# A batched matmul with a subtraction: transposes ahead of the subtract, single first loads, fewer zero matmuls, a reordered list of transfers

## Chip, cores, metric

One core of a Trainium2 chip. The metric is the device time of one execution in microseconds (us). Every run told of here is a program on one core; differences are judged with a 95% interval. "Faster" or "slower" means by more than 2%.

## The reference

```python
def setup_inputs():
    batch, m, k, n = 16, 512, 1024, 768
    return {
        "x": np.random.randn(batch, m, k).astype(np.float32),
        "weight": np.random.randn(k, n).astype(np.float32),
        "sub_value": np.random.randn(batch, m, n).astype(np.float32),
    }

def reference(x, weight, sub_value):
    return (np.matmul(x, weight) - sub_value).astype(np.float32)
```

## The kernel before

The 8192 rows of x are 64 tiles of 128. A tile is loaded as float32, cast to float16 (ScalarE, tile 1 on VectorE), transposed, multiplied with the weights into PSUM, and the subtrahend is taken off by VectorE, in place in the buffer from which the output is written. Of every six tiles, two (a "pair") are transposed by VectorE in 16 blocks, four by TensorE against an identity. SyncE issues all transfers, from one list in one order:

```python
SEGMENTS = [(0, 2), (2, 6)] + [(at, 8) for at in range(8, 64, 8)]   # which rows share a partition
N16P, NXTP = 2, 1        # buffers of a pair: cast, transposed
IDLE = 34
LEAD_TURN = 5
PER = 6

TRANSFERS = [            # kind (x, weights, subtrahend, output), first tile, tiles
    ('x', 0, 2), ('x', 2, 2), ('w', 0, 2), ('w', 2, 2), ('x', 4, 4), ('s', 0, 2), ('s', 2, 6),
    ('x', 8, 4), ('x', 12, 4), ('s', 8, 8), ('x', 16, 8), ('s', 16, 8), ('x', 24, 8),
    ('o', 0, 2), ('o', 2, 6), ('s', 24, 8), ('s', 32, 8), ('x', 32, 8), ('x', 40, 8),
    ('o', 8, 8), ('o', 16, 8), ('s', 40, 8), ('x', 48, 2), ('x', 50, 6), ('o', 24, 8),
    ('s', 48, 8), ('x', 56, 8), ('s', 56, 8), ('o', 32, 8), ('o', 40, 8), ('o', 48, 8),
    ('o', 56, 5), ('o', 61, 2), ('o', 63, 1),
]
# ... (cut)
    def idle(n):
        pe.add(lambda: nc.tensor.ldweights(idle_w, tile_position=(0, 0)), [(counter["idle"], 2)])
        for _ in range(n):
            pe.add(lambda: loaded_matmul(po_b[:, NPO - 1, 0], idle_w, idle_x, start=True, stop=True))
# ... (cut)
    idle(IDLE)           # and one more, which waits for the identity
# ... (cut)
    for mi in range(n_mt):
        for c in range(n_c):
            # ... (cut: transposes on TensorE at fixed places)
            matmuls(mi, c)
        for t in casts.get(mi, []):
            cast(t)
        finish(mi)                                   # VectorE: the subtract of tile mi
        for t in range(mi + 1, n_mt):
            if t in ON_DVE and mi == t - LEAD_TURN:
                waiting += transposes_dve(t)         # VectorE: 16 blocks of a pair
        for f in waiting[:PER]:
            f()
        del waiting[:PER]
```

The matmuls of a tile wait for its transposes and for a free one of three PSUM buffers, that is for the subtract of three tiles before.

Of the kernel before, what the change touches and what calls it, by code (L numbers as in the profile page):

```python
# [10 lines left out]
F32 = mybir.dt.float32  # L11
F16 = mybir.dt.float16

SEGMENTS = [(0, 2), (2, 6)] + [(at, 8) for at in range(8, 64, 8)]
NX, NSO = 16, 32
N16, NXT, NPT, NPO = 4, 4, 2, 3
N16P, NXTP = 2, 1
TA = 2
TURN_AT = 2
IDLE = 34  # L20
LEAD_TURN = 5
CAST_AHEAD = (6, 7, 4, 4, 3, 3)
W_ON_ACT = {(0, 0), (0, 1), (1, 0), (1, 1), (2, 0), (3, 0)}
# [2 lines left out]
ON_DVE = frozenset(range(0, 64, 6))  # L26

TRANSFERS = [
    ('x', 0, 2), ('x', 2, 2), ('w', 0, 2), ('w', 2, 2), ('x', 4, 4), ('s', 0, 2), ('s', 2, 6),
    ('x', 8, 4), ('x', 12, 4), ('s', 8, 8), ('x', 16, 8), ('s', 16, 8), ('x', 24, 8),  # L30
    ('o', 0, 2), ('o', 2, 6), ('s', 24, 8), ('s', 32, 8), ('x', 32, 8), ('x', 40, 8),
    ('o', 8, 8), ('o', 16, 8), ('s', 40, 8), ('x', 48, 2), ('x', 50, 6), ('o', 24, 8),
    ('s', 48, 8), ('x', 56, 8), ('s', 56, 8), ('o', 32, 8), ('o', 40, 8), ('o', 48, 8),
    ('o', 56, 5), ('o', 61, 2), ('o', 63, 1),
]


# [75 lines left out]
def kernel(  # L113
# [7 lines left out]
    nc = tc.nc  # L121
# [13 lines left out]
    def view(flat, at, n):  # L135

        first, size = next(one for one in SEGMENTS if one[0] <= at < sum(one))
        assert at + n <= first + size
# [8 lines left out]
    def sbuf(name, shape, dtype):  # L147
        return ctx.enter_context(nc.sbuf_tensor(name, shape, dtype)).ap()

    def psum(name, shape, dtype):  # L150
        return ctx.enter_context(nc.psum_tensor(name, shape, dtype)).ap()

    ident = sbuf("ident", [P, P], F32)
# [11 lines left out]
    idle_w = sbuf("idle_w", [P, P], F16)  # L165
    idle_x = sbuf("idle_x", [P, 512], F16)
    pt_b = psum("pt_b", [P, NPT, K], F16)
    po_b = psum("po_b", [P, NPO, 2, 512], F32)

    counter = {}  # L170
# [4 lines left out]
    def count(name):  # L175
        so_far[name] += 1
        return (counter[name], 1)

    sp, pe = Queue(nc, nc.sync), Queue(nc, nc.tensor)
# [15 lines left out]
    made = so_far["ident"]  # L195
# [3 lines left out]
    def loaded_matmul(out, weights, moving, start, stop):  # L199

        with nc.discard():
            full = nc.tensor.matmul(out, weights, moving, start=start, stop=stop).ins
        return nc.tensor.add_instruction(mybir.InstMatmult(  # L203
            name=nc.get_next_instruction_name(), engine=full.engine, ins=list(full.ins), outs=list(full.outs),
            start_tensor_calc=full.start_tensor_calc, stop_tensor_calc=full.stop_tensor_calc,
            tile_size=full.tile_size, tile_position=full.tile_position, ldweights=False,
        ))
# [8 lines left out]
    def take(pool_name, n, mi):  # L216

        b = used[pool_name] % n
        used[pool_name] += 1
        slot[pool_name, mi] = b  # L220
        before = holder.get((pool_name, b))
        holder[pool_name, b] = mi
        return b, before
# [90 lines left out]
    def cast(mi):  # L314
        assert mi in done["x"]
        done["cast"].add(mi)
        x_in = x_ring[:, mi % NX]
        first = mi - mi % 2
        waits = [landed["x", mi]]
        if first in ON_DVE:  # L320
            if mi == first:
                b, before = take("x16p", N16P, mi)
                if before is not None:
                    waits.append((counter["pair"], pair_at[before]))
            to = x16p_b[:, slot["x16p", first], mi - first]
        else:
            b, before = take("x16", N16, mi)
            if before is not None:
                waits.append((counter["turn"], turn_at[before]))
            to = x16_b[:, b]  # L330
        name = "both" if first in ON_DVE else "cast"
        if mi == 1:
            dve.add(lambda to=to, from_=x_in: nc.vector.tensor_copy(out=to, in_=from_), waits, count(name))  # L333
        else:
            act.add(lambda: nc.scalar.copy(out=to, in_=x_in), waits, count(name))  # L335
        cast_at[mi] = (name, so_far[name])
        issue()
# [27 lines left out]
    def transposes_dve(mi):  # L365

        x16 = x16p_b[:, slot["x16p", mi]].bitcast(F32).rearrange("p j (c q) -> p (j c) q", c=n_c)
        blocks = [(a, b) for a in range(P // Q) for b in range(P // Q)]

        def one(n, a, b):  # L370
            def f():
                waits = []
                if n == 0:
                    d, before = take("xtp", NXTP, mi)
                    waits.append((counter["both"], cast_at[mi + 1][1]))
                    if before is not None:
                        waits.append((counter["mul"], mul_at[before + 1]))
                xt = xtp_b[:, slot["xtp", mi]].bitcast(F32).rearrange("p j (c m) -> p (j c) m", c=n_c)
                last = n == len(blocks) - 1
                dve.add(lambda: nc.vector.transpose(  # L380
                    xt[b * Q : (b + 1) * Q, :, a * Q : (a + 1) * Q],
                    x16[a * Q : (a + 1) * Q, :, b * Q : (b + 1) * Q],
                ), waits, count("pair") if last else None)
                if last:
                    pair_at[mi] = so_far["pair"]
            return f
        return [one(n, a, b) for n, (a, b) in enumerate(blocks)]
# [33 lines left out]
    def finish(mi):  # L421
        assert mi in done["s"]
        done["finish"].add(mi)
        o = so_ring[:, mi % NSO].rearrange("p (h n) -> p h n", h=2)
        po = po_b[:, slot["po", mi]]
        dve.add(lambda: nc.vector.tensor_tensor(  # L426
            out=o, in0=po[:, :, :NS], in1=o, op=mybir.AluOpType.subtract
        ), [landed["s", mi], (counter["mul"], mul_at[mi])], count("finish"))
        finish_at[mi] = so_far["finish"]
        issue()  # L430
# [2 lines left out]


    def idle(n):
        pe.add(lambda: nc.tensor.ldweights(idle_w, tile_position=(0, 0)), [(counter["idle"], 2)])  # L436
        for _ in range(n):
            pe.add(lambda: loaded_matmul(po_b[:, NPO - 1, 0], idle_w, idle_x, start=True, stop=True))

    def transpose_tile(mi):  # L440
        for f in transposes(mi):
            f()

    def on_dve(mi):
        return mi - mi % 2 in ON_DVE

    idle(IDLE)
    pe.add(lambda: loaded_matmul(po_b[:, NPO - 1, 0], idle_w, idle_x, start=True, stop=True), [(counter["ident"], made)])
    cast(0)
    cast(1)  # L450
    for f in transposes_dve(0):
        f()
    cast(2)
    cast(3)
    for c in range(n_c):
# [7 lines left out]
    for mi in range(n_mt):  # L463
        if mi % PERIOD == 0:
            marks.append(len(pe.ops))
            pe.seen = {k: v for k, v in pe.seen.items() if k == counter["evac"].name}
        for c in range(n_c):
            if (mi % PERIOD, c) == CUT:
                marks.append(len(pe.ops))
                for t in (mi + 1, mi + 2):  # L470
                    if t < n_mt:
                        transpose_tile(t)
            matmuls(mi, c)
            if c == TURN_AT and mi % PERIOD < 2:
                transpose_tile(mi + TA)
        for t in casts.get(mi, []):
            cast(t)
        finish(mi)
        for t in range(mi + 1, n_mt):
            if t in ON_DVE and mi == t - LEAD_TURN:  # L480
                waiting += transposes_dve(t)
        for f in waiting[:PER]:
            f()
        del waiting[:PER]
    assert not todo and not waiting

    for q in (sp, pool, act, dve):
# [7 lines left out]
    last = next(one for one in left if of_o[n_mt - 1] in one["tags"])  # L495
# [36 lines left out]
```

## Time and profile before

| | before |
|---|---|
| time, median (range) | 211.25 us (211.2 to 211.36), 3 runs |
| span in the profile | 209.0 us |
| TensorE busy | 195.5 us, 94% |
| transfers | 87.03 MB, 97.5% of 16 DMA engines |
| last matmul ends | 203.5 us |
| last write has landed | 207.8 us |

The span is the profiled execution; the time is some 2 us longer. "Busy" of a matmul is modelled, so TensorE's 94% is not 94% of its peak. Beside the page, the trace keeps for each transfer the times of its 16 semaphore increments, one from each DMA engine, without the engine's name. They are quoted below as the time of the sixteenth, from the start of the span as in all views, and how far it lies behind the median of the sixteen. "The late engine" is short for the one that sent the sixteenth; that it is the same engine in every transfer is inferred from the steps between the times, not recorded. (The prediction's times of increments, and the 207.6 us for a refill in an expectation, were counted from another origin: they are 0.02 us late for the old kernel and 0.22 us late for the changed one.)

### The profile page before, as it was taken

The page shows a single profiled execution, that of the slowest core. Times are in us where ns is not written, and L with a number is a line of the kernel's source. Part 1 is how long each engine was busy: PE and PEld are TensorE (multiplying, and loading weights), DVE is VectorE, ACT ScalarE, POOL GpSimd, SP SyncE. Part 2 cuts the span into 40 slices and gives each one's busy share as a digit, 9 for nine tenths or more (in the row PEclk, how much of TensorE's full clock was granted, in tenths as well). Part 3 has the DMA queues.
Part 4 walks back from the last instruction along what each step waited for, and adds up shares of the span by engine and source line. Part 5 has one row for each costly group of instructions (what it writes and reads, how often), then busy time and mean ns, then how long its engine had stood idle before and what let it go on. Part 6 is the DMA issues. An engine that isn't in the chain of part 4 may idle for free.

```text
span 209.0 us, 2636 instructions
## 1 busy us (share of the span) xinstructions
PE 195.5 (94%) x1227; PEld 69.5 (33%) x681; DVE 139.8 (67%) x251; ACT 107.4 (51%) x112; POOL 0.9 (0%) x6
## 2 busy tenths in 40 slices
PE   6958996999899999999999999999999999999990
PEld 0003431442334334344233433424433343343420
DVE  2761679359659649929956965992993895599231
ACT  2555833764287095366277709626653752962300
POOL 1000000000000000000000000000000000000000
PEclk9999999999999999999999999999999999999998
DMA  5999999999999999999999999999999999999983
GB/s 205 424 437 417 456 418 433 455 464 397 409 481 414 341 439 440 439 445 437 426 439 426 414 442 433 409 459 411 442 437 436 439 422 423 451 419 437 425 369 151
DMA packets 5156, 87.07 MB, mean 417 GB/s; under 512 B 544, under 2 KB 544, under 8 KB 1568
## 3 DMA queue, kind: packets, MB, share of 16 engines
q1 hardware_dynamic: 5152, 87.03, 97.5%
q8 instruction: 1, 0.02, 0.0%
q14 instruction: 3, 0.02, 0.0%
HBM read 61.87 MB, written 25.17 MB: 416 GB/s over the span
## 4 chain that ended last, share of the span: by engine, by line
PE 72%; DMA 19%; DVE 3%; SPq 2%; issue 1%; DVEq 0%
PE po_b L203 65%; DMA so_ring<-in_sub_value_dram 19%; PE pt_b L353 7%; DVE xtp_b L380 2%; SPq L300 2%; DVE so_ring L426 1%; SPq L268 1%; SPq L527 0%; DVEq L57 0%; SPq L145 0%
## 5 line engine op out<-in xcount | busy, mean ns | idle before, releaser
L203 PE MATMUL po_b<-w_sb,xt_b 128*128 128x384 f16 x672 | 112.6, 326 | 0.0
L426 DVE TENSOR_TENSOR so_ring<-po_b,so_ring 128x768 f32<-128x768 f32 x64 | 61.0, 957 | 55.4 <-PE po_b L203 42.7
L380 DVE STREAM_TRANSPOSE xtp_b<-x16p_b 32x256 f32<-32x256 f32 x176 | 76.6, 435 | 3.0 <-ACT x16p_b L335 0.4
L360 ACT COPY xt_b<-pt_b 128x1024 f16<-128x1024 f16 x42 | 41.5, 1013 | 69.3 <-PE pt_b L353 68.2
L203 PE MATMUL po_b<-w_sb,xtp_b 128*128 128x384 f16 x352 | 62.7, 326 | 6.3 <-ACT w_sb L310 3.4
L406 PEld LDWEIGHTS <-xt_b 128*128 128x128 f16 x336 | 32.9, 98 | 73.5 <-issue 73.2
L335 ACT CAST x_b<-x_ring 128x1024 f16<-128x1024 f32 x42 | 41.9, 1050 | 12.6 <-DMA x_ring<-in_x_dram 12.6
L406 PEld LDWEIGHTS <-xtp_b 128*128 128x128 f16 x176 | 17.2, 98 | 50.2 <-issue 34.1
L335 ACT CAST x16p_b<-x_ring 128x1024 f16<-128x1024 f32 x21 | 21.0, 1047 | 6.0 <-DMA x_ring<-in_x_dram 6.0
L353 PE MATMUL pt_b<-ident,x_b 128*128 128x128 f32 x168 | 23.6, 273 | 0.0
L353 PEld LDWEIGHTS pt_b<-ident,x_b 128*128 128x128 f32 x168 | 20.4, 141 | 8.0 <-issue 7.3
L203 PE MATMUL po_b<-idle_x,idle_w 128*128 128x512 f16 x35 | 10.1, 461 | 1.7 <-POOL idle_x L183 1.7
L310 ACT CAST w_sb<-so_ring 128x768 f16<-128x768 f32 x6 | 4.6, 828 | 2.4 <-DMA so_ring<-in_weight_dram 2.4
L333 DVE CAST x16p_b<-x_ring 128x1024 f16<-128x1024 f32 x1 | 0.7, 694 | 3.4 <-DMA x_ring<-in_x_dram 3.4
L308 DVE CAST w_sb<-so_ring 128x768 f16<-128x768 f32 x2 | 1.0, 556 | 1.6 <-DMA so_ring<-in_weight_dram 1.6
L335 ACT ACT_TABLE_LOAD x1 | 1.3, 1283 | 0.9 <-SPq L145 0.9
L192 DVE TENSOR_TENSOR ident<-along,across 32x32 f32<-32x32 f32 x4 | 0.7, 183 | 0.1
L184 DVE MEMSET ones<- 128x32 f32 x1 | 0.1, 85 | 1.0 <-SPq L145 1.0
L436 PEld LDWEIGHTS <-idle_w 128*128 128x128 f16 x1 | 0.1, 102 | 1.7 <-POOL idle_x L183 1.7
L183 POOL MEMSET idle_x<- 128x512 f16 x1 | 0.5, 530 | 0.0
L189 DVE STREAM_TRANSPOSE across<-along 128x32 f32<-128x32 f32 x1 | 0.2, 212 | 0.0
L182 POOL MEMSET idle_w<- 128x128 f16 x1 | 0.2, 204 | 0.5 <-SPq L145 0.5
(6 smaller groups left out, 0.8 us busy)
## 6 DMA issues: line engine op xcount, KB each, us to landing
so_ring<-in_sub_value_dram SPq DMA_DIRECT2D x7, 3072.0 KB, 32.0
x_ring<-in_x_dram SPq DMA_DIRECT2D x5, 4096.0 KB, 23.7
out_dram<-so_ring SPq DMA_DIRECT2D x6, 3072.0 KB, 30.5
x_ring<-in_x_dram SPq DMA_DIRECT2D x3, 2048.0 KB, 28.1
x_ring<-in_x_dram SPq DMA_DIRECT2D x3, 1024.0 KB, 6.9
so_ring<-in_weight_dram SPq DMA_DIRECT2D x2, 1536.0 KB, 11.8
x_ring<-in_x_dram SPq DMA_DIRECT2D x1, 3072.0 KB, 23.5
so_ring<-in_sub_value_dram SPq DMA_DIRECT2D x1, 2304.0 KB, 23.7
```

Source lines behind the costliest of these rows:

```text
L192: dve.add(lambda here=here: nc.vector.tensor_tensor(out=ident[here, here], in0=along[here], in1=across[here], op=mybir.AluOpType.is_equal, ...
L203: return nc.tensor.add_instruction(mybir.InstMatmult(name=nc.get_next_instruction_name(), engine=full.engine, ins=list(full.ins), outs=lis ...
L268: sp.add(lambda here=st, there=there: nc.sync.dma_start(out=here, in_=there), then=(sem, 16))
L300: sp.add(lambda here=here, there=there: nc.sync.dma_start(out=here, in_=there), waits, (sem, 16))
L308: dve.add(lambda to=to, from_=from_: nc.vector.tensor_copy(out=to, in_=from_), [(sem, value)], count(name))
L310: act.add(lambda to=to, from_=from_: nc.scalar.copy(out=to, in_=from_), [(sem, value)], count(name))
L335: act.add(lambda: nc.scalar.copy(out=to, in_=x_in), waits, count(name))
L353: pe.add(lambda: nc.tensor.transpose(words, from_, ident), waits, count("turn") if last else None)
L360: act.add(lambda: nc.scalar.copy(out=xt_b[:, d], in_=pt_b[:, b]), waits, count("evac"))
L380: dve.add(lambda: nc.vector.transpose(xt[b * Q : (b + 1) * Q, :, a * Q : (a + 1) * Q], x16[a * Q : (a + 1) * Q, :, b * Q : (b + 1) * Q],), ...
L406: pe.add(lambda weights=weights: nc.tensor.ldweights(weights, tile_position=(0, 0)), [w for w in waits if w[0] in ready])
L426: dve.add(lambda: nc.vector.tensor_tensor(out=o, in0=po[:, :, :NS], in1=o, op=mybir.AluOpType.subtract), [landed["s", mi], (counter["mul"] ...
```

## The change

The intent: take away TensorE's two waits for the transposes of pairs 6 and 12 by putting the blocks ahead of the subtract in VectorE's program; start on tile 0 when it alone has landed; warm TensorE's clock right before its first real matmuls and not from the start; bring one block of the subtrahend forward; end with two writes for three.

```diff
-SEGMENTS = [(0, 2), (2, 6)] + [(at, 8) for at in range(8, 64, 8)]
+SEGMENTS = [(0, 1), (1, 7)] + [(at, 8) for at in range(8, 64, 8)]
-IDLE = 34
+IDLE, WARM_AT = 10, 6
@@ TRANSFERS (cut to what moves)
-    ('x', 0, 2), ('x', 2, 2), ... ('s', 0, 2), ('s', 2, 6),
+    ('x', 0, 1), ('x', 1, 1), ('x', 2, 2), ... ('s', 0, 1), ('s', 1, 1), ('s', 2, 6),
-    ('o', 0, 2), ('o', 2, 6),
+    ('o', 0, 1), ('o', 1, 7),
-    ('x', 48, 2), ('x', 50, 6), ('o', 24, 8), ('s', 48, 8),
+    ('x', 48, 2), ('s', 48, 8), ('x', 50, 6), ('o', 24, 8),
-    ('o', 56, 5), ('o', 61, 2), ('o', 63, 1),
+    ('o', 56, 6), ('o', 62, 2),
@@ the seventh transpose of pair 0 releases the zero matmuls (cut)
-    idle(IDLE)
-    pe.add(... one zero matmul more, waiting for the identity ...)
     cast(0)
     cast(1)
     for f in transposes_dve(0):
         f()
+    idle(IDLE)
@@ main loop
-        finish(mi)
         for t in range(mi + 1, n_mt):
             ...
         del waiting[:PER]
+        finish(mi)
```

## The prediction

> **What bounds the kernel now.** I read the page first, then the waits, the timeline of each engine, the stretches at the tail, and last the trace's records of packets and of semaphore increments. The page offers two candidates for the bound:
>
> ```profile
> PE 195.5 (94%) x1227; PEld 69.5 (33%) x681; DVE 139.8 (67%) x251; ACT 107.4 (51%) x112; POOL 0.9 (0%) x6
> DMA  5999999999999999999999999999999999999983
> q1 hardware_dynamic: 5152, 87.03, 97.5%
> PE 72%; DMA 19%; DVE 3%; SPq 2%; issue 1%; DVEq 0%
> ```
>
> TensorE is busy for 94%, the transfers for 97.5%, and the chain that ended last is 72% TensorE. The chain goes back through the last subtract to the last matmul. The next views show why I do not take it at its word. TensorE has only two holes after its start, both waits for a pair's transposes on VectorE:
>
> ```profile
> 34.66 2.11 PE L203 MATMUL po_b<-w_sb,xtp_b 128*128 128x384 f16 x12 [1.78 <-DVE xtp_b L380]
> 53.28 2.11 PE L203 MATMUL po_b<-w_sb,xtp_b 128*128 128x384 f16 x12 [1.11 <-DVE xtp_b L380]
> ```
>
> From 53.28 to 203.5 us TensorE has no hole. Against it stand the stretches of the tail (PE, PEld, DVE, ACT, POOL busy, then clock, DMA share, GB/s) and the issues of the last writes:
>
> ```profile
> 201.00:202.00 1.00, 1.00 (x8) 0.29 (x3) 0.89 (x1) 0.00 (x0) 0.00 (x0) 1.00 0.94 399
> 202.00:203.00 1.00, 1.00 (x8) 0.29 (x3) 0.00 (x0) 0.00 (x0) 0.00 (x0) 1.00 0.48 203
> 203.00:204.00 1.00, 0.49 (x4) 0.00 (x0) 0.47 (x1) 0.00 (x0) 0.00 (x0) 1.00 0.99 415
> 204.00:205.00 1.00, 0.00 (x0) 0.00 (x0) 0.49 (x1) 0.00 (x0) 0.00 (x0) 1.00 0.60 249
> 205.00:206.00 1.00, 0.00 (x0) 0.00 (x0) 0.00 (x0) 0.00 (x0) 0.00 (x0) 1.00 0.74 301
> 206.00:207.00 1.00, 0.00 (x0) 0.00 (x0) 0.00 (x0) 0.00 (x0) 0.00 (x0) 1.00 0.39 154
> ```
>
> The mean DMA share sinks after 202, as if most of the 16 DMA engines waited for TensorE. But the engines differ. Each transfer raises its semaphore 16 times, once from each engine, and the trace keeps the times. At 37.5 us 15 increments of a transfer come within 0.4 us and the sixteenth 1.2 us later; from then on one increment is always late, by 1.9 us against the median at 95 us and by 2.25 us at 205 us. The last write but two has 13 increments by 202.9 and its last at 205.0; the next is complete at 206.84, the last at 207.77, the span ending at 209.0. The last write is issued at 204.5, when the late engine still has 2.3 us of earlier work. So **one late DMA engine, never out of work from 2.0 to 207.4 us, sets the end**; TensorE's last matmul has about 2.3 - 0.9 = 1.4 us to spare, for 0.9 us is what that engine needs for its share of the last 384 KB (1.2 us from issue to first data is covered by that work).
>
> **What the Trainium skill says.** (1) "DMA: Bandwidth & Descriptors", section "Why a DMA increments its semaphore by 16 and not by 1": a transfer is split over up to 16 engines that finish independently. The trace agrees: 34 transfers, 544 increments. (2) Same page, "Where 436 GB/s comes from": 435 GB/s for the 16 ports together. The trace shows 418 to 439 GB/s in stretches of 20 us and more, so no reordering can raise the rate. (3) "Runtime: NRT & Kernel Launch", section "Instruction fetch mechanics": instructions are refilled by DMA in blocks of 16 KiB. The trace has one such packet of 16,384 B at 32.8 us, just before the late engine falls back; that it is the cause I infer. (4) "TensorE: Matmul & The Clock Gate", Part 1: the clock doubles after about 3.4 us of activity in a free-running window. The trace agrees roughly: the zero matmuls start every 426 ns from 1.7 until 6.4 us (11 of them), then every 216 ns. A gap of 2.6 us before the real matmuls did not lose the clock.
>
> **The change part by part.**
>
> *Zero matmuls.* 35 took 10.11 us, before 11.8 us, when TensorE had nothing else. The ten now start at the seventh transpose of pair 0: cast of tile 1 by 6.6, then 7 x 0.449 us, so about 9.8. At 426 ns they end by 14.1, or by 13.7 if the clock rises at 13.3. The transposes end about 13.8, the first weight casts at 13.6. So real matmuls start about 14.1 instead of 14.38. Cold, the first eight would take 8 x 0.32 = 2.6 us and end at 16.7; but the third weight block is cast only at 16.6 in any case (0.83 us wait before 16.67 in the old trace). Cost 0 to 0.1 us; TensorE's busy time falls by about 6 us, off the path.
>
> *Single loads.* Tile 0 lands near 4.7 instead of 5.9, tile 1 still at 5.9, since bytes decide. Transposes begin at 6.65 instead of 6.99: 0.3 us, swallowed by the same weight wait. Subtract block 0 lands 0.9 us earlier, near 21.5.
>
> *Transposes first.* VectorE's program was subtract 1, six transposes, subtract 2 (waiting until 27.99 for its block), six, subtract 3, four. Now: six (casts ready at 22.65) to 25.3, subtract 1 to 26.3, six to 29.0, subtract 2 to 29.95, four to 31.8. TensorE wants pair 6 at 32.7 and gets it: 1.7 us gained. Subtract 3 then ends at 32.75, just when tile 6 needs its PSUM buffer; subtract 2 is as close. For pair 12 the same argument removes 1.1 us, but meanwhile tiles 10 and 11 wait for casts behind the load that landed at 38.9 (0.4 us back), and tile 11 for subtract 8 (0.2 us back). TensorE stands about **2.1 us earlier** at tile 12.
>
> Then comes a load that the change does not move:
>
> ```profile
> 105.48 1.99 ACT L335 CAST x_b<-x_ring 128x1024 f16<-128x1024 f32 x2 [4.91 <-DMA x_ring<-in_x_dram]
> 107.27 0.60 PE L353 MATMUL pt_b<-ident,x_b 128*128 128x128 f32 x4
> ```
>
> Tile 32 lands at 105.47 on the late engine; its cast ends at 106.5; TensorE transposed it at 107.27. TensorE can be only about 0.7 us early here. The rest of the 2.1 us becomes a wait of about 1.4 us. After this nothing else is tight (tile 56 has some 4 us). The last matmul ends near 202.8 instead of 203.5.
>
> *Transfers.* The same 87.03 MB, one transfer more. From the trace's packets, 24,576 B take 913 ns and two of 3,072 B take 242 ns against 234 for one of 6,144: the split costs some 0.1 us per engine. Block 48 of the subtrahend moves ahead of x tiles 50 to 55: the wait of 3.27 us of its subtract goes, but TensorE never waited for it. x 50 lands near 154.5 instead of 147.2 and is wanted after 158.
>
> *Tail.* Five, two and one tiles become six and two. The late engine has the same bytes in the same order, so it ends at 207.77 again. The others get their two tiles at 203.8 + 1.2 and need 8 packets x 234 ns = 1.9 us: about 207.0, in the shadow of the late engine.
>
> **Sum:** 0.3 + 1.7 + 1.1 on TensorE, less 0.9 and less 1.4, leaves 0.7 us of TensorE and nearly 0 us of time. I take 211.0, 0.25 below the old time, for the late engine can only by luck be better placed.
>
> **Rivals.** *TensorE is the bound after all:* its holes, 1.78 + 1.11 = 2.9 us, come off, giving 208.4. The 72% of the chain speaks for it; tile 32 and the late increments speak against. Even this is 1.4%, not 2%. *Another engine is late, or less so:* 25 instructions fewer shift the refills; without lateness the ordinary engines' 207.0 binds, giving 210.5; with more, 211.7. I give this a third. *The clock is not up in time:* ten matmuls for 4.3 us barely fill a window; half speed for another 3.4 us costs 1.7 us, of which the spare 1.4 us takes most: up to 212. *The bigger last write is exposed:* if TensorE gains nothing it ends at 207.7, level with now; 0.4 us more at worst, 211.6. *A PSUM wait replaces the transpose wait* (subtracts 2, 3, 8 come 1 to 2.7 us later): costs some of the 2.1 us, which tile 32 would take anyway.
>
> **Range and chances.** Most of the weight lies between the floor without lateness (210.5) and the exposed tail (211.6), a little wider downward for the intent: 210.3 to 211.6. A change of 2% needs 4.2 us, more than all holes together: faster 0.01, slower 0.01.
>
> **What would show each step.** Right: no wait of matmuls for xtp_b near 33 and 51 us; a new TensorE wait of about 1.4 us near 105 for the cast of tile 32; TensorE's busy time near 189.5; the last matmul at 202.5 to 203.1; the sixteenth increment of the last write near 207.7, about 2 us after the median of the write before. Wrong: tile 32 landing much before 105, or a last write whose 16 increments come together, with the span shortened as TensorE's end; then TensorE was the bound.

## The result

The changed kernel takes 211.19 us (210.96 to 211.47, 4 runs) against 211.22 us (210.99 to 211.36, 4 runs) for the old one; ratio 1.0, interval 0.9983 to 1.0018. The ratios are not quite the ratios of the medians. In five more rounds later it was 211.02 us, ratio 0.9994 (0.9981 to 1.0007).

The page of the changed kernel: busy times, granted clock by slice, transfers, chain.

```profile
PE 191.7 (92%) x1202; PEld 70.1 (34%) x681; DVE 140.1 (67%) x251; ACT 107.5 (51%) x112; POOL 0.9 (0%) x6
PEclk9996999999999999999999999999999999999996
q1 hardware_dynamic: 5296, 87.03, 97.7%
PE 89%; DMA 7%; SPq 1%; DVE 0%; ACT 0%; issue 0%
```

The transfers are as busy as ever; the chain now names TensorE for 89%, though the time is the same. The fourth slice of the clock, 15.7 to 20.9 us, reads 6: TensorE ran at half speed for a part of it. The timeline of TensorE shows where, and that both waits for transposes are gone (start, duration, instruction, in brackets the wait before it):

```profile
9.52 4.45 PE L203 MATMUL po_b<-idle_x,idle_w 128*128 128x512 f16 x10 [9.52 <-DVE xtp_b L380]
13.86 0.56 PE L203 MATMUL po_b<-w_sb,xtp_b 128*128 128x384 f16 x2
...
17.58 1.44 PE L203 MATMUL po_b<-w_sb,xtp_b 128*128 128x384 f16 x4 [1.04 <-ACT w_sb L310]
...
35.22 2.11 PE L203 MATMUL po_b<-w_sb,xtp_b 128*128 128x384 f16 x12
...
52.57 2.11 PE L203 MATMUL po_b<-w_sb,xtp_b 128*128 128x384 f16 x12
...
106.62 0.66 PE L353 MATMUL pt_b<-ident,x_b 128*128 128x128 f32 x4
```

Tile 6 starts 0.56 us later than in the old kernel (35.22 for 34.66), tile 12 0.71 us earlier (52.57 for 53.28), and TensorE keeps most of this to the end: its last matmul ends at 202.9, 0.6 us earlier. Four real matmuls at 17.58 take 1.44 us where the old kernel's took 0.81. The tail by stretches, columns as before:

```profile
201.00:202.00 1.00, 1.00 (x8) 0.32 (x4) 0.29 (x1) 0.00 (x0) 0.00 (x0) 1.00 0.86 369
202.00:203.00 1.00, 0.89 (x6) 0.11 (x2) 0.07 (x1) 0.00 (x0) 0.00 (x0) 1.00 0.99 424
203.00:204.00 1.00, 0.00 (x0) 0.00 (x0) 0.89 (x1) 0.00 (x0) 0.00 (x0) 1.00 1.07 461
204.00:205.00 1.00, 0.00 (x0) 0.00 (x0) 0.00 (x0) 0.00 (x0) 0.00 (x0) 1.00 0.73 313
205.00:206.00 1.00, 0.00 (x0) 0.00 (x0) 0.00 (x0) 0.00 (x0) 0.00 (x0) 0.59 1.00 418
206.00:207.00 1.00, 0.00 (x0) 0.00 (x0) 0.00 (x0) 0.00 (x0) 0.00 (x0) 0.50 0.87 363
```

TensorE and VectorE are done by 204, and the transfers run on until past 207 as in the old kernel. The increments say who they wait for:

```
write of tiles        sixteenth increment, us   behind the median
before  48 to 55      200.40                    2.22
        56 to 60      204.98                    2.24    4.58 us later
        61 and 62     206.81                    1.81    1.83 us later
        63            207.75                    1.02    0.94 us later
after   48 to 55      200.44                    2.47
        56 to 61      205.90                    0.45    5.46 us later
        62 and 63     207.74                    0.46    1.84 us later
```

The packets of the old trace take 0.91 us for the share of one tile in one engine (24,576 B in 913 ns). So the steps of the late engine, 4.58, 1.83 and 0.94 us, are 5, 2 and 1 tiles of pure work: it did not stand idle between them. In the changed kernel 5.46 and 1.84 us are 6 and 2 tiles, again without a gap. The others waited: their median is only 0.45 us ahead at the end, because the write of six tiles is now issued at 198.7, after the subtract of tile 61, where the write of five was issued at 196.3.

"One late engine" is too simple. For tiles 48 to 55 of the old kernel the fifteenth increment is 1.97 us behind the median and the sixteenth 2.22, and at the end they are 0.26 us apart. The packets agree: of the 16 that are in progress at once through most of the execution, 3 are left at 202.6 us, 2 at 206.5 and 1 from 207.2 on. Two engines were late by nearly the same time, and a third by 1.1 us.

### The profile page after: what moved, and what is told of

Read it like the earlier page. It is cut to its first block, busy times and chain, and to the rows that moved or that the text cites. A ratio compares the mean times of both kernels' runs of the same rounds, so it can differ in the third digit from the quotient of the medians.

```text
span 209.0 us, 2622 instructions
## 1 busy us (share of the span) xinstructions
PE 191.7 (92%) x1202; PEld 70.1 (34%) x681; DVE 140.1 (67%) x251; ACT 107.5 (51%) x112; POOL 0.9 (0%) x6
## 4 chain that ended last, share of the span: by engine, by line
PE 89%; DMA 7%; SPq 1%; DVE 0%; ACT 0%; issue 0%
PE po_b L203 80%; PE pt_b L353 9%; DMA so_ring<-in_weight_dram 7%; SPq L300 1%; DVE so_ring L426 0%; ACT w_sb L310 0%; SPq L268 0%; SPq L526 0%; SPq L145 0%
## 5 line engine op out<-in xcount | busy, mean ns | idle before, releaser
L203 PE MATMUL po_b<-w_sb,xtp_b 128*128 128x384 f16 x352 | 64.5, 330 | 1.7 <-ACT w_sb L310 1.7
L406 PEld LDWEIGHTS <-xt_b 128*128 128x128 f16 x336 | 32.9, 98 | 73.5 <-issue 73.2
L353 PE MATMUL pt_b<-ident,x_b 128*128 128x128 f32 x168 | 24.1, 276 | 0.0
L203 PE MATMUL po_b<-idle_x,idle_w 128*128 128x512 f16 x10 | 4.4, 632 | 9.5 <-DVE xtp_b L380 9.5
```

Source lines behind the costliest of these rows:

```text
L203: return nc.tensor.add_instruction(mybir.InstMatmult(name=nc.get_next_instruction_name(), engine=full.engine, ins=list(full.ins), outs=lis ...
L353: pe.add(lambda: nc.tensor.transpose(words, from_, ident), waits, count("turn") if last else None)
L406: pe.add(lambda weights=weights: nc.tensor.ldweights(weights, tile_position=(0, 0)), [w for w in waits if w[0] in ready])
```

## The experiments

Twelve kernels ran, each given here as an edit of one of the two. Rounds of the old kernel gave 211.21 to 211.23 us.

### The old zero matmuls in the changed kernel

```diff
-IDLE, WARM_AT = 10, 6        # and the wait for the seventh transpose
+IDLE = 34                    # all at the start, as before, and one more
```

> The changed kernel with one part undone: the 35 zero matmuls at the start as before. Theory (one late DMA engine sets the end, TensorE has slack): the real matmuls run at full clock from about 14 us, TensorE stands some 2 us earlier at tile 12 than in the old kernel (51.2 against 53.28), waits about 1.4 us for the cast of tile 32 near 105 us, and the time stays at 211.2 within 0.3. Rival (TensorE is the bound, and the changed kernel merely lost at the start what it gained): the 2.5 us of half clock come back, and the time falls by 1.4 to 2.5 us, to 208.7 to 209.8.

Measured: 211.45 us, ratio 1.0005 (0.9991 to 1.0019). It did not test what it was meant to. Its zero matmuls ended at 11.2 us, the gap to the real ones was 2.96 us, and the clock fell:

```profile
PEclk9995899999999999999999999999999999999997
```

The last matmul ended at 203.7, as in the old kernel. The 35 zero matmuls are thus no surer than the ten (see below).

### More work for TensorE at the very end

```diff
+            if (mi, c) == (n_mt - 1, n_c - 1):
+                pe.add(lambda: nc.tensor.ldweights(idle_w, tile_position=(0, 0)), [])
+                for _ in range(5):          # 15 in the second run
+                    pe.add(lambda: loaded_matmul(pt_b[:, 0].bitcast(F32), idle_w, idle_x, start=True, stop=True))
             matmuls(mi, c)
```

> The kernel before, with 5 zero matmuls of 512 columns into a free PSUM bank ahead of the last eight real matmuls: the last matmul ends 5 x 0.216 = 1.1 us later (204.6 for 203.5). Theory (late DMA engine, 1.4 us to spare for TensorE): time unchanged within 0.3 us. Rival (TensorE's chain, as the chain of waits shows it): 1.1 us longer, 212.3.

> The same with 15 zero matmuls: 3.24 us more on TensorE. Theory: the spare 1.4 us take some, 1.8 us longer, 213.0; rival: 3.2 us longer, 214.4. With the run of 5 it also measures the spare time.

Measured: 211.38 us, ratio 1.0005 (0.9991 to 1.0018), for five, and 213.36 us, ratio 1.01 (1.0085 to 1.0116), for fifteen. The lines of TensorE in the run with fifteen, then with five:

```profile
202.65 3.40 PE L203 MATMUL pt_b<-idle_x,idle_w 128*128 128x512 f16 x15
205.89 0.81 PE L203 MATMUL po_b<-w_sb,xt_b 128*128 128x384 f16 x4
```

```profile
202.56 1.24 PE L203 MATMUL pt_b<-idle_x,idle_w 128*128 128x512 f16 x5
203.64 0.81 PE L203 MATMUL po_b<-w_sb,xt_b 128*128 128x384 f16 x4
```

Of 15 x 0.216 = 3.24 us only 2.14 show in the time, and of 1.08 us nothing that the interval separates from zero. So **TensorE had 3.24 - 2.14 = 1.1 us to spare**, 0.8 to 1.4 by the interval. The increments agree: with fifteen, the late engine goes from 206.97 for tiles 61 and 62 to 210.04 for tile 63, 3.08 us for 0.91 us of work, so it waited 2.17 us; with five it waited 0.2 us. This is the direct proof that the chain of waits, which names TensorE for 72%, does not name the bound.

### Fewer bytes

```diff
-    ('s', 56, 8)
+    ('s', 56, 7)      # tile 63 subtracts what its buffer held before; wrong on purpose
```

> The kernel before, loading 7 of the last 8 tiles of the subtrahend (the last tile subtracts stale data, a wrong result on purpose): 384 KB less of the 87 MB, nothing less for TensorE or VectorE. Theory: every DMA engine has 24 KB less, 0.91 us at its measured rate, so 0.6 to 0.95 us shorter, about 210.4 (the ordinary engines' last write, issued when TensorE is done, then comes close to binding). Rival (TensorE): no change.

Measured: 210.47 us, ratio 0.9963 (0.9949 to 0.9977), wrong result as meant. TensorE, VectorE and ScalarE had no less to do, only the 16 DMA engines had 0.91 us less each, and the time fell by 0.75 us. The last write's sixteenth increment comes at 206.88, 0.2 us behind the median: the late engine and the others nearly meet.

### No gap at all before the real matmuls

```diff
+    pe.add(lambda: nc.tensor.ldweights(idle_w, tile_position=(0, 0)), [(counter["idle"], 2)])
+    for _ in range(34):                      # beside the ten of the change
+        pe.add(lambda: loaded_matmul(po_b[:, NPO - 1, 0], idle_w, idle_x, start=True, stop=True))
     cast(0)
```

> The run with 35 zero matmuls did not test what it was to test: the clock fell again in the gap before the real matmuls. Here the changed kernel has 34 zero matmuls at the start and its own ten at the seventh transpose, so that no gap is left. Both theories expect full clock for the real matmuls from 14 us on. Theory (late DMA engine): TensorE some 2 us earlier than the old kernel at tile 12 (51.2 for 53.28), a wait near 105 us of about 1.4 us for the cast of tile 32, time 211.2 within 0.3. Rival (TensorE is the bound): 208.7 to 209.8.

Measured: 210.96 us, ratio 0.9994 (0.9973 to 1.0016). Now the clock held. TensorE in this run:

```profile
17.78 0.81 PE L203 MATMUL po_b<-w_sb,xtp_b 128*128 128x384 f16 x4 [1.00 <-ACT w_sb L310]
...
51.42 2.11 PE L203 MATMUL po_b<-w_sb,xtp_b 128*128 128x384 f16 x12
...
105.77 0.65 PE L353 MATMUL pt_b<-ident,x_b 128*128 128x128 f32 x4 [0.20 <-ACT x_b L335]
```

Tile 12 starts at 51.42, 1.86 us before the old kernel, close to the 51.2 foreseen. The wait for the cast of tile 32 is there, but small: TensorE loses 0.4 us at this place, not 1.4, for tile 32 landed at 104.7. The last matmul ends at 202.0, **1.5 us before the old kernel's, and the time does not move**. The write of tile 63 has its sixteenth increment at 207.45, 1.0 us behind the median.

### The order of VectorE alone

```diff
-        finish(mi)
         for t in range(mi + 1, n_mt):
             ...
+        finish(mi)
```

> The kernel before with one part of the change alone: transposes of a pair ahead of the subtract. Theory: the waits of 1.78 and 1.11 us for the transposes vanish, TensorE is at most 0.7 us earlier from tile 32 on, and the time stays at 211.2 within 0.2. Rival (TensorE): up to 2.9 us faster, 208.4.

Measured: 211.26 us, ratio 0.9998 (0.9984 to 1.0012). The waits for transposes vanish; two others come:

```profile
30.68 2.76 PE L203 MATMUL po_b<-w_sb,xt_b 128*128 128x384 f16 x16 [0.49 <-DVE so_ring L426]
106.94 0.66 PE L353 MATMUL pt_b<-ident,x_b 128*128 128x128 f32 x4 [0.93 <-ACT x_b L335]
```

The first is tile 5 waiting for the subtract of tile 2, which now stands behind twelve blocks; the second is the cast of tile 32, whose load landed at 105.8. Tile 12 started at 51.27, 2.0 us early; the last matmul ended 0.3 us early. The late engine ended 1.35 us behind the median.

### The list of transfers alone

```diff
 # SEGMENTS and TRANSFERS of the changed kernel, all else as before
```

> The kernel before with the new list of transfers and the single first tiles alone. Theory: both waits for transposes stay, TensorE ends at about 203.5 as before, the late engine at 207.8 to 208.0, time 211.2 within 0.3. Rival (the new order of transfers is what costs, and the order of VectorE gains the same): 212 or more. It also shows whether the lateness from 9.5 us on, new in the changed kernel, belongs to the single first loads.

Measured: 211.29 us, ratio 1.0004 (0.9989 to 1.0019). Both waits for transposes stay:

```profile
35.75 2.11 PE L203 MATMUL po_b<-w_sb,xtp_b 128*128 128x384 f16 x12 [1.87 <-DVE xtp_b L380]
53.68 2.11 PE L203 MATMUL po_b<-w_sb,xtp_b 128*128 128x384 f16 x12 [0.42 <-DVE xtp_b L380]
```

Here the increments of the last write all come within 0.1 us of the median, at 208.4 (the profiled execution took 211.78 us, 0.5 above the median of this kernel): without the time that the new order gives TensorE, the tail of six and two tiles has no spare left. The third weight block is used at 17.67 us for 16.67, because one engine is late by 1.27 us from 9.4 us on. All six kernels with the new list show this; the eight with the old list have 0.3 us or less until 33.

### Keeping work from one engine

```diff
+            if kind == "o" and at >= 61:
+                # two transfers: partitions 0 to 119, then 120 to 127
```

> The kernel before, with the last two writes (tiles 61, 62 and tile 63) each cut into 120 partitions, which fifteen engines share, and the remaining 8 partitions, shared by eight. Theory (one late engine sets the end): if the late engine is the one that the 120 partitions leave out, it is done at about 205 and the others at 207.0 to 207.2, 0.5 to 0.8 us shorter; if it is among the fifteen, 0.1 to 0.4 longer for two more transfers. Rival (TensorE): 0.3 longer in any case, for the last piece is issued 0.4 us later.

Measured: 212.46 us, ratio 1.0061 (1.0047 to 1.0075). Nothing is told about the late engine. Packets of 6,144 B of these writes took 283 ns in the median for 234 otherwise, so most of the engines were slowed; the last increment came at 208.4, and the span closed 2.1 us after it where all the others closed 1.3 us after theirs. As an idea for this kernel it failed. Nor could leaving out one engine have gained the 0.5 to 0.8 us hoped for: the second-latest was only 0.26 us before it in the old kernel.

### One transfer more

```diff
-    ('s', 56, 8)
+    ('s', 56, 4), ('s', 60, 4)
```

In the second run together with the order of VectorE.

> The kernel before with one transfer more: the last eight tiles of the subtrahend in two halves, the first loads in pairs as before. In all kernels with the old list a 16,384 B refill of instructions runs near 33 us and one engine is 1.4 us late from the next landing on; in those with the new list the refill runs near 207.6 and the lateness comes from 9.5 us instead. Theory A (the refill makes the engine late, and the length of the list places the refill): the refill moves to the end, no step of lateness at 39 us, the late engine some 1.2 us nearer to the others, and the time falls by 0.5 to 0.9 us, to 210.4. Theory B (the place of the refill depends on something else in the list, or does not matter): lateness of 1.4 us at 39 us as ever, time 211.2 within 0.2.

> The same list of transfers with the transposes ahead of the subtract: the candidate for a version better than both. Theory A: the late engine is less late and TensorE ends 0.7 us earlier, so 0.6 to 1.4 us shorter, 209.8 to 210.6. Theory B: 211.2 within 0.2.

Measured: 211.36 us, ratio 1.001 (0.9996 to 1.0024), and 211.25 us, ratio 1.0003 (0.9989 to 1.0018). The refill stayed (33.3 and 34.6 us), and so did the step at 39 us (1.36 and 1.44 us). One half of theory A falls: the length of the list does not place the refill. What places it stays open. The other half, that the refill makes an engine late, was not tested by this run; the traces bear on it (see the last point on the prediction below).

### Once more, and the old tail

```diff
-    ('o', 56, 6), ('o', 62, 2),
+    ('o', 56, 5), ('o', 61, 2), ('o', 63, 1),       # second run only
```

> The changed kernel once more, unaltered, for five rounds and a second trace. If the half clock of the first real matmuls belongs to the ten zero matmuls, it shows again: real matmuls of 0.24 us start to start until about 20 us, TensorE 0.5 us late at tile 6 (35.2 for 34.66) and 0.7 early at tile 12; if it was the phase of the clock's window, the matmuls of the second trace may be at full speed and TensorE 2 us early at tile 12. Time 211.2 within 0.2 either way.

> The changed kernel with the last writes of the old one (five, two and one tiles for six and two). Theory: the late engine has the same bytes in the same order and ends at 207.8 to 208.0, the others now 1 us or more before it, since the write of five tiles does not wait for the sixth: time 211.2 within 0.2. Rival (the new tail costs what TensorE gained): 0.4 to 0.7 us shorter, 210.6.

Measured: 211.02 us, ratio 0.9994 (0.9981 to 1.0007), and 211.08 us, ratio 0.9991 (0.9976 to 1.0007). They were run on another chip. In both the clock held, with the same ten zero matmuls. The unaltered kernel's second trace:

```profile
9.48 3.81 PE L203 MATMUL po_b<-idle_x,idle_w 128*128 128x512 f16 x10 [9.48 <-DVE xtp_b L380]
...
17.89 0.81 PE L203 MATMUL po_b<-w_sb,xtp_b 128*128 128x384 f16 x4 [1.01 <-ACT w_sb L310]
...
34.19 2.11 PE L203 MATMUL po_b<-w_sb,xtp_b 128*128 128x384 f16 x12
...
51.53 2.11 PE L203 MATMUL po_b<-w_sb,xtp_b 128*128 128x384 f16 x12
```

Tile 12 starts 1.75 us before the old kernel and the last matmul ends 1.4 us before it; the time is the same within the interval. With the old tail, the late engine ends at 208.00, 2.36 us behind the median and 0.8 us behind the fifteenth increment: here it alone sets the end. No kernel of the series beats both by more than its interval, except the one with fewer bytes.

## Why the prediction was right

The time (211.0 for 211.19) and its cause hold; several steps on the way were of the wrong size and did not matter. The one result did not decide it: TensorE ended only 0.6 us earlier, and a time shorter by as much, 210.6, would have lain in the range too. The experiments decided it.

- **Late DMA work, and not TensorE, as the bound: shown.** Delaying TensorE costs nothing up to about 1 us, advancing it by 1.5 us gains nothing that can be measured, and taking 0.91 us of bytes from each engine gains 0.75 us. Wrong was "one": the prediction's own 13 increments by 202.9 leave three late ones, not one.
- **The same end, 207.74 for 207.77: in part luck.** The lateness had another origin than foreseen. The refill that was to cause it moved to 207.4 us, as a rival had feared (with the list, and not with the 25 instructions: with the list alone it runs at 208.1 us), and lateness of about the same size, 1.0 us, came with the first loads, at 9.3 us.
- **The spare time was mis-sized:** 1.4 us foreseen, 1.1 measured (0.8 to 1.4). I took from the late engine's 2.3 us of earlier work the 0.9 us of its last share, which it has to move in any case. What has to come off, by the old trace's packets, is the 0.84 us from issue to first data on an engine that waits, and the 0.33 us from an engine's last data to its increment, for the 2.3 us were counted to the increment: 2.3 - 0.84 - 0.33 = 1.1.
- **Zero matmuls, "cost 0 to 0.1 us": wrong for the first trace.** The records of the granted clock have it full at 14.0, half from 17.5 and full again from 20.9 us. The cost allowed for cold first matmuls only; a lost window, 1.7 us, stood among the rivals. Tile 2 started at 23.95 us against 22.66 in the second trace, where the clock held: 1.3 us, though not in the time. The "gap of 2.6 us did not lose the clock" was the luck of that trace.
- **Single loads, "swallowed by the same weight wait": wrong in sign.** I took the third weight block as ready at 16.6 "in any case". With the new list one engine is late from 9.3 us on, and that block is used at 17.58 us, 17.89 in the second trace and 17.67 with the list alone, for 16.67 before: 0.9 to 1.2 us lost at the start, not 0.
- **Transposes first: shown where the clock held.** Tile 12 came 1.9 and 1.75 us early (2.1 foreseen); in the first trace, 0.7, the clock having taken the rest. With the order alone it came 2.0 us early, and the PSUM wait feared for tile 5 was 0.5 us.
- **The wait of 1.4 us at tile 32: half right.** With the order alone it was 0.93 us, with a full clock in the changed kernel 0.4, in the first trace nothing that the view of waits lists for a matmul (0.4 us for a weight load): TensorE was only 0.7 us early there. So the last matmul at 202.9 (202.8 foreseen) was a right number by a wrong road. The landing of tile 32 varied between 104.7 and 106.0 us over the runs.
- **The tail: right in its end, too loose in its slack.** I looked at the last write only. The write of six tiles, issued 2.4 us later than the one of five, let the others run dry, so that they finish only 0.45 us before the late engine. So the new tail uses up most of what the order gives; with the old tail the others are 2.36 us ahead. The rival of the exposed tail is close, and with the list alone it is level.
- **Busy time of TensorE:** 189.5 foreseen, 191.7 measured; where the clock held, in the second trace, it was 189.7. (The sum's own terms leave 0.8 us of TensorE, not 0.7, and by the line at 34.66 TensorE wanted pair 6 at 32.9, not 32.7; neither matters.)
- **The refill as cause of the lateness: right for the old list, not for the new.** In all eight kernels with the old list a step of 1.2 to 1.3 us comes right after the 16,384 B packet of instructions near 33 us, and the packets show how. In the old kernel's trace it runs for 0.93 us, and nearly all that time 15 packets of transfers are in progress and not 16: one engine moves no data. A packet of 16,384 B that starts as it ends takes 1.11 us for the usual 0.61. That makes 0.93 + 0.50 = 1.43 us; the sixteenth increment of the next landing is 1.44 us behind. All eight traces have this pair of packets. Three packets of instructions of 8,192 B in every trace (in the old kernel's at 50.5, 85.0 and 141.4 us) do the same for 0.31 us each, and 0.24 to 0.53 us in the packet after. In the six with the new list the 16,384 B packet runs at 206.9 to 208.5 us and one engine is late all the same, from 9.3 to 9.6 us on. What places the refill, and what makes an engine late there, the runs do not tell.

## What to carry to other kernels

A chain of waits that runs through TensorE, and a mean DMA share that sinks at the end, can hide that one or two of 16 DMA engines are still working without a pause: compare the last of a transfer's increments with their median, and see whether its steps are bytes over rate. Before an edit on a busy engine, measure its spare time by adding work to it, and the rival's by taking bytes away; here two runs decided it. A gain for an engine with spare time is not lost through a mistake in the edit; it was never on the path.

## What the Trainium skill lacked or had wrong

- "TensorE: Matmul & The Clock Gate", Part 1: the clock falls after at least one idle window of about 3.4 us. The clock records agree with steps of 3.4 us, but idle is too strict as this row of its table has it (a later section of the Part tells of a kernel that loses the clock by short idling, without a measure): it fell after gaps of 2.96, 3.03 and 3.37 us (three of the ten kernels with 35 zero matmuls at the start and nothing after; the other seven had gaps of 1.9 to 2.9 us), and in the changed kernel with no gap over 1.04 us, in a window busy for 0.54. How busy is enough stays open: the three falls with 35 zero matmuls followed windows busy for 0.22 to 0.39, but the old kernel kept the clock with two windows in a row busy for 0.54 and 0.46.
- "Runtime: NRT & Kernel Launch", section "Instruction fetch mechanics": crossing a block is mostly hidden. For a core bound by its transfers it is not: in eight of eight kernels with a refill packet of 16,384 B near 33 us, that packet takes 0.93 us of one DMA engine, the transfer's packet after it 0.50 us more than usual, and an engine is 1.2 to 1.3 us later from the next landing on.
- "DMA: Bandwidth & Descriptors": its section on the 16 increments says that engines finish independently, not by how much. Its section "Latency and other measured facts" has engines 7 and 15 as usually slower, for descriptors written by software; these transfers are issued by SyncE, and the records do not name the engine. Here the latest was 1.5 to 3.3 us behind the median in the last quarter of every run before the last writes, about 1% of the span, and that was the bound. No page says what writes over 15 engines cost: packets of 6,144 B took 283 ns in the median for 234 in the one run that had them.
